# Turning two 64-wide heads with one 128x128 transposition, and moving the first key projections to other PSUM banks

## The chip, the cores and the metric

The kernel runs on one core of one Trainium2 chip. The metric is the time of one execution on the device in microseconds (us); what is compared is the median over runs of the same program.

## The reference

Two layers of an encoder block on 512 tokens of width 1024, all in float32. Each layer is a gated feed-forward, a token mixer, a second gated feed-forward, and a gated embedding step, with a layer norm after each. The change is inside the token mixer, and there in the gated delta rule with 4 heads of dimension 128, which works on chunks of 64 tokens:

```
gdn_qkv = silu(causal_dwconv(gdn_qkv, gdn_conv_w))      # 4 taps along the tokens
g_q = l2_normalize(g_q) * GDN_HEAD_DIM ** -0.5
g_k = l2_normalize(g_k)
...
u, w  = t_inv @ (v * beta), t_inv @ (k * beta * exp(gcum))
qk    = (q @ k.T) * decay
step:  v_new = u - w @ state
       o     = q_dec @ state + qk @ v_new
       state = state * g_last + k_dec.T @ v_new
```

The same mixer also holds a stick-breaking attention (4 heads of 64) and a short gated convolution; their outputs are concatenated and projected.

## The kernel before

**Number formats.** Every large product is done as three float16 products (`mm3`, lines 256 to 258): operands are split into a high and a low float16 half, and high x high, high x low and low x high are accumulated in PSUM. Weights arrive by DMA as float32 into `raw` (3 buffers) and are split by one ScalarE and one VectorE instruction per half tile (lines 139 and 140) into a buffer `w`.

**The mixer (`mix_body`).** Tokens are kept along the free dimension: `proj_T` computes a projection as 128 channels x 512 tokens in one PSUM bank, 24 matmuls of 512 columns each. For the delta rule each head's projection passes through `conv` (one ScalarE instruction, line 616, and three on VectorE, line 619), which reads the PSUM bank of the projection, and then through `silu` (ScalarE, line 546). The result has the head's 128 channels on the partitions and 512 tokens = 8 chunks of 64 on the free axis. The state update needs it the other way round, with tokens on the partitions. `turn` (line 700) does that for a pair of heads (`hp` names the pair, `e` the head in it): for each chunk, head 0 goes to partitions 0 to 63 and head 1 to partitions 64 to 127 of one PSUM tile, by a float32 matmul with the identity for each head and chunk, 16 matmuls per pair. There are six turns per layer: two for the keys (`pkt`), two for the values (`pvt`), two for the queries (`pqt`). Behind them ScalarE and VectorE read the turned tiles (lines 717, 718, 721 for keys; 949 for values; 962, 963 for queries).

Keys and queries stay in `kq`, since the products of a chunk with itself (`pm`, line 749, and `pqk`, line 976) and with the state (`pks`, line 1007) read them with channels on the partitions. Values live only until their turn: their `silu` is done in place in the buffer that `conv` filled.

**PSUM.** There are three pools: `acc` (2 banks, the output of `proj_T`), `bank` (3) and `bank2` (3). The first key projections (`early`, two heads, name `pk`) go to `acc`, as do the four `pv` products before them, the next two key projections, and the attention's projections `psb` behind those.

**SBUF.** In the mixer, pool `w1` has 5 buffers under the tag `w`; the split weights, the attention's `hl`, and `zT` share them. A load whose buffer is not free waits. `conv` tiles have 5 buffers under the tag `cv`.

**Order.** A planner orders every engine's instructions once, at compile time, by program order as priority and by its own estimates of when each will be ready. TensorE then runs its queue strictly in that order. The planner fills TensorE with whatever product is ready: around the key turns these are the `psb` matmuls, and around the value and query turns the next projection's matmuls and the steps of a triangular inverse (`levels`, line 916). A few places are tied by hand: `silu` waits for the last exponential before it (`tables_end`), to save loads of activation tables.

**The gate chain.** The gate values `g` go through a chain from `pab` (line 631) through VectorE and ScalarE to `pe` (line 654), then `pl` (line 672), the decays `E` and `ET`, and only then the first `silu` of the keys.

Of the kernel before, what the change touches and what calls it, by code (L numbers as in the profile page):

```python
# [10 lines left out]
F32 = mybir.dt.float32  # L11
# [6 lines left out]
P = 128  # L18
# [15 lines left out]
class Block:  # L34
# [511 lines left out]
        self.silu_end = self.nc.scalar.activation(out, a, AF.Silu, scale=scale)  # L546
        self.after(self.silu_end, self.tables_end)

    def proj_T(self, w, xT, c, name):

        ps = self.acc(name)
        for k in range(KD):
            self.mm3(
                ps, [w[:, h, k, c * P : (c + 1) * P] for h in range(2)],
                [xT[:, h, k] for h in range(2)], k == 0, k == KD - 1,
            )
        return ps

    def mix_body(self, i, j, last, pool):
        nc, ins, xT, x = self.nc, self.ins, self.xT, self.x  # L560
# [3 lines left out]
        H, C, NC, G16 = 4, 64, 2 * NT, NT * 4  # L564
        halves = [slice(64 * e, 64 * e + 64) for e in range(2)]
# [22 lines left out]
        ps = self.bank2("ps_rows", (P, 64))  # L588
# [24 lines left out]
        def conv(ps, c):  # L613
            a = pool.tile([P, S], F32, name="conv", tag="cv", bufs=5)
            w = lambda tap: cw[:, tap * 12 + c : tap * 12 + c + 1]
            nc.scalar.activation(a, ps, AF.Copy, scale=w(3))
            for tap in (2, 1, 0):
                d = 3 - tap
                nc.vector.scalar_tensor_tensor(
                    a[:, d:], ps[:, : S - d], w(tap), a[:, d:], op0=ALU.mult, op1=ALU.add  # L620
                )
            return a

        w = self.load_cols(w_in, OFF_K)
        early = [conv(self.proj_T(w, xT, e, "pk"), 4 + e) for e in range(2)]


        pab = self.bank("pab", (P, NT, 2, 4))
        for c in range(2):
            for e in range(2):  # L630
                nc.tensor.matmul(
                    pab[halves[e], :, c], self.ident[:, halves[c]], ab[:, :, e::2],
                    start=True, stop=True,
# [32 lines left out]
        for a in range(2):  # L666
# [13 lines left out]


        kq2 = [
            self.w2.tile([P, 2, NC, 2, C], F32, name="kq", tag="w") for _ in range(2)
        ]
        kq = [kq2[h // 2][:, h % 2] for h in range(H)]
        bv = self.w2.tile([P, NC, 2, P], F32, name="bv", tag="w")
        kdec = self.w2.tile([P, NC, 2, P], F32, name="kdec", tag="w")
        ssk = pool.tile([P, NC, 2], F32, name="ssk")
# [2 lines left out]
        def bc(cols, n=P):  # L691
            m = cols.shape[-1]
            return cols.rearrange("p (m a) -> p m a", a=1).to_broadcast([P, m, n])

        def turn(src, name):

            pts = [self.bank(name, (P, 4, P)) for _ in range(2)]
            for n in range(NC):
                for e in range(2):
                    nc.tensor.matmul(  # L700
                        pts[n // 4][halves[e], n % 4], src(e, n), self.ident, start=True, stop=True
                    )
            return [(pt, slice(4 * b, 4 * b + 4)) for b, pt in enumerate(pts)]

        def chunks(v):
            return v.rearrange("p (n c) -> p n c", c=C)

        for hp in range(2):
            if hp == 1:
                w = self.load_cols(w_in, OFF_K + 256)  # L710
            for e in range(2):
                h = 2 * hp + e
                a = conv(self.proj_T(w, xT, e, "pk"), 4 + h) if hp else early[e]
                self.silu(kq[h][:, :, 0], chunks(a))
            for pt, ns in turn(lambda e, n: kq[2 * hp + e][:, n, 0], "pkt"):
                sq = self.t2("sq", (P, 4, P))
                nc.scalar.activation(sq, pt, AF.Square)
                nc.vector.tensor_reduce(
                    ssk[:, ns, hp], sq, axis=mybir.AxisListType.X, op=ALU.add
                )  # L720
                nc.vector.tensor_tensor(
                    kdec[:, ns, hp], pt, bc(eg[:, 1].rearrange("p (n h) -> p n h", h=2)[:, ns, hp]),
                    op=ALU.mult,
                )
# [76 lines left out]
        for hp in range(2):  # L801
            ps = self.proj_T(wq, xT, hp, "psb")
            for e in range(2):
                own, other, h = rows_of(e), rows_of(1 - e), 2 * hp + e
# [4 lines left out]
        for hp in range(2):  # L809
            ps = self.proj_T(wk, xT, hp, "psb")  # L810
            for e in range(2):
                own, other, h = rows_of(e), rows_of(1 - e), 2 * hp + e
# [9 lines left out]
        for n_u, (h, kts) in enumerate(((0, (2, 3)), (0, (1,)), (1, (2, 3)), (0, (0,)), (1, (1,)), (2, (2, 3)),  # L822
                       (1, (0,)), (2, (1,)), (3, (2, 3)), (2, (0,)), (3, (1,)), (3, (0,)))):
            hp, e = divmod(h, 2)
            es = slice(64 * e, 64 * e + 64)
            off = {k: 256 * (k == 3) for k in kts}
            n = 512 if kts == (0,) else 384
            zb = self.bank2("zb")[:, :n]
            zt = {k: zb[:, off[k] : off[k] + S - k * P] for k in kts}
            for k in kts:  # L830
# [3 lines left out]
                    start=k == kts[0], stop=False, skip_group_check=True,  # L834
# [15 lines left out]
            pair = hlb[:, n_u % 4]  # L850
# [4 lines left out]
            for k in reversed(kts):  # L855
                for k2 in range(NT - 1, k - 1, -1):
                    lhs = self.ntri if k2 == k else self.nones
                    for q in range(2):
                        nc.tensor.matmul(
                            zt[k][:, (k2 - k) * P :], lhs, hls[h][k2][:, q], start=False,  # L860
                            stop=k2 == k and q == 1, skip_group_check=True,
# [5 lines left out]
            for k in kts:  # L867
# [3 lines left out]
                    start=k == 2, stop=k == 0, skip_group_check=True,  # L871
# [7 lines left out]
        hb, a = ([self.t2(n) for _ in range(2)] for n in ("hb", "sca"))  # L879
        for c in range(2):  # L880
            nc.scalar.activation(hb[c], self.proj_T(wh, xT, c, "psh"), AF.Copy, scale=IWS)
        for c in range(2):
# [3 lines left out]
            w = lambda tap: cw[:, 48 + 2 * tap + c : 49 + 2 * tap + c]  # L886
# [52 lines left out]
        level = levels()  # L939
        for hp in range(2):  # L940
            w = self.load_cols(w_in, OFF_V + 256 * hp)
            pair = []
            for e in range(2):
                next(level, None)
                a = conv(self.proj_T(w, xT, e, "pvv"), 8 + 2 * hp + e)
                self.silu(a, a)
                pair.append(chunks(a))
            for pt, ns in turn(lambda e, n: pair[e][:, n], "pvt"):
                nc.vector.tensor_tensor(bv[:, ns, hp], pt, bc(rk[:, 1, ns, hp]), op=ALU.mult)


# [1 line left out]
        for hp in range(2):  # L953
            w = self.load_cols(w_in, OFF_Q + 256 * hp)
            for e in range(2):
                h = 2 * hp + e
                next(level, None)
                a = conv(self.proj_T(w, xT, e, "pqq"), h)
                self.silu(kq[h][:, :, 1], chunks(a))
            for pt, ns in turn(lambda e, n: kq[2 * hp + e][:, n, 1], "pqt"):  # L960
                sq = self.t2("sq", (P, 4, P))
                nc.scalar.activation(sq, pt, AF.Square)
                nc.vector.tensor_reduce(
                    ssq[:, ns, hp], sq, axis=mybir.AxisListType.X, op=ALU.add
                )
# [17 lines left out]
        for hp in range(2):  # L983
            w = self.load_cols(w_in, OFF_Z + 256 * hp)
# [192 lines left out]
```

## Time and profile before

| | us |
|---|---|
| median of 3 runs | 2031.88 |
| lowest, highest run | 2029.93, 2032.16 |
| the profiled execution, its own time | 2031.65 |
| its span, first to last instruction | 2029.9 |

The profile shows one execution. What lies around the span is 1.75 us. TensorE appears as two rows, PE for the matmuls and PEld for the loading of the stationary operand; DVE is VectorE, ACT is ScalarE, POOL is GpSimd, and SPq is the queue that issues the DMAs. PEclk is the clock that TensorE was granted as a share of full speed, and over the whole span it is 0.997. A matmul's row shows its whole latency, so the spacing of starts, not the duration, is what one costs in a stream.

### The profile page before, as it was taken

Reading aid. Unit: us, or ns where it says so; the run is one execution under the profiler, and the core shown is the slowest. Engines: PE = TensorE matmul, PEld = TensorE weight load, DVE = VectorE, ACT = ScalarE, POOL = GpSimd, SP = SyncE. Lnnn points to the kernel's source line nnn. Section 1 sums busy time; section 2 is a strip of 40 time slices with the busy share of each in tenths; the row PEclk is TensorE's granted clock in tenths of the full one; section 3 lists DMA queues with packets and bytes.
Section 4 is the critical chain, followed back from the end, with each engine's and each line's share of the span. In section 5 each row is a group of like instructions: output and inputs, shape, how many; then the busy total and the mean of one; then the engine's idle time right before and its main releaser. Section 6 shows DMA issues by size and latency. Waiting matters only on the chain.

```text
span 2029.9 us, 33679 instructions
## 1 busy us (share of the span) xinstructions
PE 1983.4 (98%) x14346; PEld 1289.0 (64%) x14346; DVE 1523.3 (75%) x2347; ACT 874.2 (43%) x1295; POOL 64.0 (3%) x84
## 2 busy tenths in 40 slices
PE   7999999999999999999999999999999999999998
PEld 5677686545545686776467686855455466776853
DVE  7995866775479986958897867577755798967686
ACT  6453352454244453543364443434533354543431
POOL 1000000100000000000000000002000000000000
PEclk9999999999999999999999999999999999999999
DMA  7533320431044443433324333222311624433221
GB/s 218 195 112 107 97 85 1 126 77 63 1 167 124 126 127 106 121 104 125 125 80 129 104 119 89 64 65 66 94 42 43 207 64 146 125 104 84 94 73 42
DMA packets 245361, 205.19 MB, mean 101 GB/s; under 512 B 20846, under 2 KB 225500, under 8 KB 245212
## 3 DMA queue, kind: packets, MB, share of 16 engines
q1 hardware_dynamic: 245212, 203.05, 32.6%
q8 instruction: 112, 1.84, 0.4%
q14 instruction: 37, 0.30, 0.0%
HBM read 200.14 MB, written 2.88 MB: 100 GB/s over the span
## 4 chain that ended last, share of the span: by engine, by line
PE 79%; DVE 12%; ACT 5%; DMA 2%; issue 1%; SPq 1%; POOL 0%; DVEq 0%; ACTq 0%
PE po L258 7%; PE po L256 7%; PE po L257 7%; PE pA L256 6%; PE pA L258 6%; PE pA L257 6%; PE pB L258 3%; PE pB L257 3%; PE pB L256 3%; DVE wq L140 3%; DVE w L140 2%; ACT w L139 2%; ACT wq L139 1%; PE pC L258 1%; PE pC L256 1%; PE pC L257 1%
## 5 line engine op out<-in xcount | busy, mean ns | idle before, releaser
L140 DVE SCALAR_TENSOR_TENSOR wq<-f,wq 128x1024 f16<-128x1024 f32 (+1 forms) x240 | 333.9, 1395 | 19.0 <-ACT wq L139 15.7
L139 ACT ACTIVATE wq<-f 128x1024 f16<-128x1024 f32 (+1 forms) x240 | 279.5, 1191 | 126.1 <-PE pB L258 83.2
L139 ACT ACTIVATE w<-raw 128x1024 f16<-128x1024 f32 (+1 forms) x196 | 193.8, 1032 | 264.6 <-PE po L258 226.3
L256 PE MATMUL po<-w,hT 128*128 128x512 f16 x704 | 266.7, 379 | 3.7 <-ACT hT L286 1.5
L256 PE MATMUL pA<-xS,wq 128*128 128x256 f16 x960 | 261.6, 272 | 6.8 <-ACT up L407 5.3
L257 PE MATMUL po<-w,hT 128*128 128x512 f16 x704 | 266.5, 379 | 0.0
L258 PE MATMUL po<-w,hT 128*128 128x512 f16 x704 | 264.3, 379 | 1.9 <-DVE hT L287 1.9
L258 PE MATMUL pA<-xS,wq 128*128 128x256 f16 x960 | 261.6, 273 | 0.0
L257 PE MATMUL pA<-xS,wq 128*128 128x256 f16 x960 | 261.6, 273 | 0.0
L140 DVE SCALAR_TENSOR_TENSOR w<-raw,w 128x1024 f16<-128x1024 f32 (+1 forms) x196 | 230.0, 1193 | 36.4 <-ACT w L139 36.4
L257 PEld LDWEIGHTS <-wq 128*128 128x128 f16 x2240 | 219.1, 98 | 42.1 <-issue 11.7
L453 DVE TENSOR_TENSOR f<-f 128x512 f32<-128x512 f32 x320 | 218.4, 686 | 28.1 <-DMA f<-in_ffn_w_in 23.0
L256 PEld LDWEIGHTS <-wq 128*128 128x128 f16 x2240 | 219.1, 98 | 30.1
L258 PEld LDWEIGHTS <-wq 128*128 128x128 f16 x2240 | 219.1, 98 | 27.5
L472 DVE SCALAR_TENSOR_TENSOR x_tok<-po,x_tok 128x512 f32<-128x512 f32 x144 | 97.5, 685 | 82.4 <-PE po L258 82.3
L256 PEld LDWEIGHTS <-hT 128*128 128x128 f16 x704 | 68.8, 98 | 85.2 <-ACT hT L286 9.9
L258 PEld LDWEIGHTS <-hT 128*128 128x128 f16 x704 | 68.0, 98 | 84.8 <-DVE hT L287 5.3
L395 DVE TENSOR_TENSOR sg<-pB,sg 128x256 f32<-128x256 f32 x80 | 33.6, 420 | 117.5 <-PE pB L258 117.5
L257 PEld LDWEIGHTS <-hT 128*128 128x128 f16 x704 | 68.9, 98 | 76.9 <-issue 1.4
L392 ACT ACTIVATE sg<-pA 128x256 f32<-128x256 f32 x80 | 30.6, 382 | 194.1 <-PE pA L258 194.1
L257 PEld LDWEIGHTS <-w 128*128 128x128 f16 x640 | 62.9, 98 | 63.1 <-issue 16.4
L256 PEld LDWEIGHTS <-w 128*128 128x128 f16 x640 | 62.7, 98 | 61.4 <-issue 6.2
(289 smaller groups left out, 3872.0 us busy)
## 6 DMA issues: line engine op xcount, KB each, us to landing
f<-in_ffn_w_in SPq DMA_DIRECT2D x160, 512.0 KB, 5.1
raw<-in_ffn_w_out SPq DMA_DIRECT2D x44, 1024.0 KB, 6.1
raw<-in_mix_w_in SPq DMA_DIRECT2D x28, 1024.0 KB, 5.3
raw<-in_mix_w_out SPq DMA_DIRECT2D x8, 1024.0 KB, 4.9
raw<-in_ple_w_gate SPq DMA_DIRECT2D x8, 1024.0 KB, 7.5
raw<-in_ffn_w_in SPq DMA_DIRECT2D x6, 1024.0 KB, 5.0
ln_gb<-in_ln_g SPq DMA_DIRECT2D x8, 512.0 KB, 3.6
ln_gb<-in_ln_b SPq DMA_DIRECT2D x8, 512.0 KB, 5.1
```

Source lines behind the costliest of these rows:

```text
L139: self.nc.scalar.activation(hi, raw, AF.Copy, scale=WS),
L140: self.nc.vector.scalar_tensor_tensor(lo, raw, WS, hi, op0=ALU.mult, op1=ALU.subtract),
L256: nc.tensor.matmul(ps, a[0], b[0], start=first, stop=False, **k)
L257: nc.tensor.matmul(ps, a[0], b[1], start=False, stop=False, **k)
L258: nc.tensor.matmul(ps, a[1], b[0], start=False, stop=last, **k)
L392: nc.scalar.activation(half(new.sg, 1), new.A, AF.Copy)
L395: nc.vector.tensor_tensor(half(old.sg, 1), old.B, half(old.sg, 1), op=ALU.add)
L453: nc.vector.tensor_tensor(f[:, to], f[:, a], f[:, b], op=ALU.add)
L472: self.nc.vector.scalar_tensor_tensor(xs, po, scale, xs, op0=ALU.mult, op1=ALU.add)
```

## The change

Three things are edited.

1. `kq2`, which held two heads one after the other (head, chunk, key or query, token), is laid out as chunk, key or query, head, token. The two heads of a pair then lie side by side for each chunk: 128 adjacent columns. For the values a new tile `vp` of the same kind is taken from `w1`, tag `w`, one per pair, and `silu` writes there instead of in place.
2. `turn` issues one `nc.tensor.transpose` per chunk, on 128 columns, instead of two matmuls with the identity on 64 columns each. What lands in PSUM is the same, in the same place.
3. `proj_T` takes an optional `bank`, and the first two key projections go to `bank2` instead of `acc`.

```
-    def proj_T(self, w, xT, c, name):
-        ps = self.acc(name)
+    def proj_T(self, w, xT, c, name, bank=None):
+        ps = (bank or self.acc)(name)
...
-        early = [conv(self.proj_T(w, xT, e, "pk"), 4 + e) for e in range(2)]
+        early = [conv(self.proj_T(w, xT, e, "pk", self.bank2), 4 + e) for e in range(2)]
...
-            self.w2.tile([P, 2, NC, 2, C], F32, name="kq", tag="w") for _ in range(2)
+            self.w2.tile([P, NC, 2, 2, C], F32, name="kq", tag="w") for _ in range(2)
         ]
-        kq = [kq2[h // 2][:, h % 2] for h in range(H)]
+        kq = [kq2[h // 2][:, :, :, h % 2] for h in range(H)]
...
             pts = [self.bank(name, (P, 4, P)) for _ in range(2)]
             for n in range(NC):
-                for e in range(2):
-                    nc.tensor.matmul(
-                        pts[n // 4][halves[e], n % 4], src(e, n), self.ident, start=True, stop=True
-                    )
+                nc.tensor.transpose(pts[n // 4][:, n % 4], src(n), self.ident)
...
-            for pt, ns in turn(lambda e, n: kq[2 * hp + e][:, n, 0], "pkt"):
+            for pt, ns in turn(lambda n: kq2[hp][:, n, 0].rearrange("p e c -> p (e c)"), "pkt"):
...
-            pair = []
+            pair = self.w1.tile([P, NC, 2, C], F32, name="vp", tag="w")
             for e in range(2):
                 next(level, None)
                 a = conv(self.proj_T(w, xT, e, "pvv"), 8 + 2 * hp + e)
-                self.silu(a, a)
-                pair.append(chunks(a))
-            for pt, ns in turn(lambda e, n: pair[e][:, n], "pvt"):
+                self.silu(pair[:, :, e], chunks(a))
+            for pt, ns in turn(lambda n: pair[:, n].rearrange("p e c -> p (e c)"), "pvt"):
...
-            for pt, ns in turn(lambda e, n: kq[2 * hp + e][:, n, 1], "pqt"):
+            for pt, ns in turn(lambda n: kq2[hp][:, n, 1].rearrange("p e c -> p (e c)"), "pqt"):
```

## Rows read from the trace of the kernel before

**Rows 1.** The page, busy time by engine: us, share of the span, instructions.

```profile
PE 1983.4 (98%) x14346; PEld 1289.0 (64%) x14346; DVE 1523.3 (75%) x2347; ACT 874.2 (43%) x1295; POOL 64.0 (3%) x84
```

**Rows 2.** Windows: length; busy us of PE, PEld, DVE, ACT, POOL; PEclk, DMA, GB/s.

```profile
370.00:372.80 2.80, 0.70 (x10) 0.31 (x8) 2.77 (x6) 0.69 (x1) 0.00 (x0) 0.98 0.14 17
372.80:376.20 3.40, 3.39 (x9) 1.24 (x10) 3.17 (x8) 2.39 (x6) 0.00 (x0) 0.52 0.96 297
404.00:416.00 12.00, 12.00 (x59) 5.38 (x57) 5.23 (x16) 2.96 (x5) 4.77 (x4) 1.00 0.16 23
416.00:440.00 24.00, 23.41 (x123) 10.64 (x122) 21.92 (x47) 17.56 (x29) 0.00 (x0) 1.00 0.34 100
480.00:540.00 60.00, 60.00 (x582) 33.22 (x581) 28.03 (x39) 17.82 (x26) 0.00 (x0) 1.00 0.08 29
580.00:610.00 30.00, 28.63 (x165) 13.67 (x166) 21.26 (x36) 13.00 (x20) 2.21 (x3) 1.00 0.43 151
976.00:978.00 2.00, 2.00 (x19) 1.84 (x18) 2.00 (x3) 2.00 (x4) 0.00 (x0) 1.00 0.44 117
```

**Rows 3.** Timeline of PE, layer 1, around the second key pair's first projection.

```profile
370.29 0.41 PE L631 MATMUL pab<-ab,ident 128*64 128x16 f32 x8
372.81 0.61 PE L256 MATMUL pk<-xT,w 128*128 128x512 f16 x1 [2.11 <-DVE conv L619]
...
376.15 0.38 PE L258 MATMUL pk<-xT,w 128*128 128x512 f16 x1
...
378.53 0.29 PE L654 MATMUL pe<-g,uin 128*128 128x16 f32 x2
```

**Rows 4.** Timeline of PE, layer 2, the same place.

```profile
1376.52 0.39 PE L256 MATMUL pk<-xT,w 128*128 128x512 f16 x1 [1.11 <-DVE conv L619]
```

**Rows 5.** Chain that ended last, turns of layer 1: start us, us, what.

```profile
391.13 2.35 PE pkt L700 x32
393.48 0.32 PE psb L257
...
394.88 1.96 PE pkt L700 x29
...
490.02 0.58 PE pvt L700 x4
...
494.16 1.89 PE pvt L700 x28
```

**Rows 6.** Instructions of tile `pkt`: count, ns min/median/max, first and last start us, forms.

```profile
L700 PE MATMUL pkt<-ident,kq x128: 272/273/324, 391.1 to 1399.0; 128*64 128x128 f32 x128
```

**Rows 7.** Instructions of tile `ps_t`, the turned tokens elsewhere in the kernel.

```profile
L220 PE MATMUL ps_t<-ident,x_tok x256: 272/273/448, 4.7 to 1979.2; 128*128 128x128 f32 x128
L223 ACT ACTIVATE xT<-ps_t x64: 573/597/616, 5.8 to 1979.7; 128x512 f16<-128x512 f32 x64
```

**Rows 8.** Timeline of PE around one block of eight such transpositions.

```profile
1005.25 0.38 PE L258 MATMUL pgate<-w,xT 128*128 128x512 f16 x1
1005.47 1.04 PE L220 MATMUL ps_t<-ident,x_tok 128*128 128x128 f32 x8
1006.34 0.38 PE L256 MATMUL pp<-w,pT 128*128 128x512 f16 x1
```

**Rows 9.** Line 546, `silu`: count, ns min/median/max, first and last start us.

```profile
L546 ACT ACTIVATE kq<-conv x16: 613/629/631, 390.3 to 1541.5; 128x512 f32<-128x512 f32 x16
L546 ACT ACTIVATE conv<-conv x8: 629/629/630, 488.1 to 1511.5; 128x512 f32<-128x512 f32 x8
```

**Rows 10.** Timeline of PE at the end of the first value projection, layer 1.

```profile
489.64 0.38 PE L258 MATMUL pvv<-xT,w 128*128 128x512 f16 x1
```

**Rows 11.** Timeline of ACT, the next splits of weights after that.

```profile
556.29 3.90 ACT L139 ACTIVATE w<-raw 128x1024 f16<-128x1024 f32 x4
```

**Rows 12.** Timeline of DVE, the last step of `g`, layer 1.

```profile
376.52 0.17 DVE L646 TENSOR_TENSOR g<-g,nega 128x16 f32<-128x16 f32 x1
```

**Rows 13.** DMA issues: engine, count, KB each, median us to landing.

```profile
raw<-in_mix_w_out SPq DMA_DIRECT2D x8, 1024.0 KB, 4.9
```

## The prediction

> **What bounds the kernel now.** I read the page first: PE is busy for 98% of the span [rows 1], so an edit counts by what it does to PE's queue and by whether another engine is close behind it. The windows show that stage by stage, inside the mixer, where all edits are. In the value and query stretch PE has not one idle microsecond of 60 while DVE works 28 and ACT 18 [rows 2]: what is cut from PE there should come off the end. Elsewhere the cover is thinner. Behind the key turns PE is full for 12 us with DVE under half busy, but from 416 to 440 DVE is at 21.9 of 24 and PE already idles 0.6; from 580 to 610 PE idles 1.4 [rows 2]. Last, the one large wait: in layer 1 PE stands for 2.11 us before the second key pair, waiting for `conv` on DVE to let go of an `acc` bank, and runs the next matmuls at a granted 0.52 [rows 2, 3]. In layer 2 the same wait is 1.11 us, and no slow stretch follows it [rows 4].
>
> **Part 1, the turns.** `turn` issues 2 pairs x 8 chunks x 2 heads = 32 matmuls per name and layer, 64 in both; the trace holds 128 for `pkt` [rows 6]. So each float32 matmul with the identity is two PE instructions, and a turn is 32. `ps_t` is what the new form looks like: 64 tiles of four transpositions, and 256 instructions for these 256 [rows 7]: one each. A turn goes from 32 to 8.
>
> Old price, from the chain: a key turn in one piece holds PE 2.35 us, and the float16 matmul behind it takes 0.32 instead of 0.22, so 2.45. The second key turn has 29 of its instructions in 1.96, 0.0676 each, hence 2.16 for 32; more float32 work follows, so no dearer exit. A value turn runs in two pieces, 4 and 28 instructions: 0.58 + 1.89, and 0.10 at the exit, 2.57 [rows 5]. The other value and query turns repeat that pattern, four in all; the last is followed by float32 work, 0.10 less. Per layer: 2.45 + 2.16 + 4 x 2.57 - 0.10 = 14.8 us.
>
> New price: eight transpositions start at 1005.47, 0.22 behind the start of the float16 matmul ahead of them, which is that matmul's own spacing, and the next float16 matmul starts at 1006.34 [rows 8]. So they hold PE 0.87 us, without entry or exit. Six make 5.2. Twice per layer (`pm`, `pqk`) other float32 work now pays the 0.10 entry that the turn paid: 0.2. Saved: 14.8 - 5.2 - 0.2 = 9.4 us per layer, 18.8 in both.
>
> Bounds: the nearest row has the same type, the same 128 columns and the same identity, so the size is good to some tenths per turn; at 1.04 us, the time of the block with its tail [rows 8], it is 12 x 0.17 = 2.0 less, 16.8. Not better than 18.8, unless the planner also places things better.
>
> **What the clock does in a turn.** Sixteen transpositions (two such blocks) fill most of 976 to 978, and the clock granted there is 1.00 [rows 2]; the matmul behind the block of rows 8 starts on time. The Trainium skill, "TensorE: Matmul & The Clock Gate", section "Part 4: PE-mode transpose", says against this change that transpose mode does not count as busy for the clock gate, so that full clock does not engage in it. By this trace eight or sixteen in a row do not lower the granted clock; by the page, each turn might bring a stretch at the lower level. I take the trace and keep the other as a rival.
>
> **What the turns wait for.** A transposition needs both heads' `silu`, where the early 4 instructions needed only one. The 28 already wait for the second head, so the block sits where they sat and PE has nothing new to wait for; the 0.58 just disappears. The `silu` count is unchanged, and its duration is 629 ns both for values in place and for keys into a strided tile [rows 9], so 0. Readers of the turned tiles find the same layout: 0. No DMA is added and none is moved past another on SP's queue; POOL gets nothing.
>
> **The new tile.** `vp` takes one of five `w1` buffers, twice per layer. When the first value head's `silu` starts (488.1), the weights of both value pairs, both query pairs and the first z pair can hold all five, and the first to come free is that of the value projection whose last matmul starts at 489.64 [rows 9, 10] and ends at 490.02. `silu` could thus start 1.9 us later. Behind it on ACT stands the second head's first `conv` step, which waits for that same matmul; it can be pushed by one `silu`, 0.63 us, and then the second `silu` and the turn by as much. Worst case 0.6 per layer, 1.2 in all; nothing if the planner swaps the two; I take 0.6. Later takers are far off: the next split of weights comes at 556 [rows 11], when both `vp` are long free. The `conv` buffers come free earlier, which nothing here waits for.
>
> **Part 2, the banks.** With the first pair in `bank2`, the second pair's `acc` banks hold only `pv` results evicted long before, and the wait for `conv` goes: 2.11 us in layer 1, 1.11 in layer 2 [rows 3, 4]. Layer 1 also gets back the slow stretch: from 372.81 to 376.15 eight matmul spacings took 3.34 us at a granted 0.52, the lower of the two levels, 1.2 GHz [rows 2, 3]; at 0.215 each they take 1.72, so 1.62. Sum 2.11 + 1.62 + 1.11 = 4.8 us.
>
> What is late next there: `pe` needs `g`, which DVE finishes at 376.69 [rows 12]. PE reached `pe` at 378.53 [rows 3], some 20 matmuls, 4.3 us at full clock, behind the start of the second pair. If the planner leaves `pe` that far behind, PE now gets there at about 370.7 + 4.3 = 375.0 and stands 1.7 us, and in layer 2 most of the 1.1 comes back too. But it places by its own times, and 10 us of ready matmuls (two projections, 48 x 0.215) can stand ahead of `pe`. So 2 to 4.8, and I take 4.8. Were the cover gone, it would be 2.
>
> **Sum.** -18.8 - 4.8 + 0.6 = -23.0 us. The profiled execution took 2031.65 by its own time and 2029.9 by its span, the median of the runs is 2031.88, 0.2 above. So 2031.9 - 23.0 = 2008.9: 2009 us, in the profile a span near 2007.
>
> **Rivals.**
>
> *DVE becomes the bound behind the keys.* PE reaches 416 earlier by the two key turns and the wait: (2.45 - 0.87) + (2.16 - 0.97) + 3.7 = 6.5 us in layer 1 and 2.8 + 1.1 = 3.9 in layer 2. If the stretch at 21.9 of 24 on DVE [rows 2] cannot follow, up to 10.4 us come back as waits before the attention's products. For: DVE's share there. Against: from 404 to 416 DVE is idle 6.8 of 12 us [rows 2] and can take work earlier. Time if all is lost: 2019; half: 2014.
>
> *The wait moves to `pe`.* Part 2 gives 2 instead of 4.8: 2012; if it gives nothing, 2014.
>
> *The transpositions let the clock fall.* If each of 12 turns brought a stretch like the one after the 2.11 us wait, 1.62 us each, 19.4 us would be given back: 2028, inside what cannot be told from no change. Against: the granted 1.00 in rows 2.
>
> *Slower: the buffer pool pushes the output weights behind the state loop.* If the planner gives freed `w1` buffers to `vp` and lets the four `mix_w_out` tiles queue behind them, a tile that lands late is exposed on PE with a transfer of 4.9 us [rows 13] and its split, for which four ACT halves took 3.9 [rows 11], so some 2 for one tile: 7 us. One per layer is 14 and still leaves a gain; from 1.6 per layer (23 us) it decides, and two per layer give 2037. For: PE already idles 1.4 us between 580 and 610 [rows 2]. Against: the splits begin at 556, some 40 us after the last `vp` is free.
>
> **Chances.** As forecast, 2004 to 2012: 0.62. DVE bound behind the keys, 2012 to 2019: 0.13. Wait at `pe`, 2011 to 2014: 0.11. Clock: 0.04. Slower: 0.04. Better than 2004, because the new order also closes some of the small waits: 0.06. A difference of 0.2%, 4 us, is about what a measurement of this kernel can tell from no change. The first three and the last are all faster by more, 0.92; the clock rival is no change, 0.04; slower 0.04. The range takes in the first three cases and leaves out the tails: 2003 to 2020, of which the likeliest case alone is 2004 to 2012.
>
> **What the profile after should show.** One instruction per transposition: 96 under the three names on the line of `turn`, in blocks of 8 that hold PE 0.87 us, with float16 spacing on both sides. No early piece of 4. The second key pair starting within 0.3 us behind `pab` in both layers, with a granted clock of 1.00 after it. PE's matmul count down by 288. PE still full from the values to the queries, and that stretch shorter by some 6.6 us per layer. I would be wrong if PE waits longer for `g`, for `silu` at a turn, or for attention splits (`hl`) than now; a planner's order that has shifted elsewhere can add or take a few microseconds that none of these terms foresee.

## The result and the profile after

The changed kernel takes 2017.18 us in the median of 4 runs (2016.35 to 2021.14), against 2031.65 for the kernel before, measured beside it: a ratio of 0.9934, 95% interval 0.9917 to 0.9951. It is faster, and the time lies inside the range, but 8 us above the 2009 forecast. The profiled execution took 2017.74 by its own time, 2016.0 by its span; the pair of profiled executions differs by 13.9 us where the sum said 23.0. Nine microseconds are missing, and the rows show where to look.

The page after, busy time by engine, answers [rows 1]:

```profile
PE 1966.5 (98%) x14058; PEld 1274.0 (63%) x14058; DVE 1524.1 (76%) x2347; ACT 871.4 (43%) x1295; POOL 65.7 (3%) x84
```

PE has 288 matmuls less, as forecast, and 16.9 us less work. The span fell by 13.9 only, so PE idles 3.0 us more than before.

The timeline of PE around the first value turn answers [rows 5], the instructions of the tile `pkt` behind it [rows 6]:

```profile
491.51 0.38 PE L258 MATMUL pvv<-xT,w 128*128 128x512 f16 x1
491.73 1.06 PE L700 MATMUL pvt<-ident,vp 128*128 128x128 f32 x8
492.72 0.45 PE L914 MATMUL pq<-TU,Ms 64*64 64x64 f32 x8
```

```profile
L700 PE MATMUL pkt<-ident,kq x32: 272/273/329, 389.6 to 1389.9; 128*128 128x128 f32 x32
```

There is one instruction per transposition (32 in `pkt` over both layers, 96 under the three names), in one block of 8 per turn, with no early piece of 4 and no wait. But the block's price is 0.99 us from its start to the next matmul's start, not 0.87. Five of the six turns of a layer are followed by small float32 tiles (`pm`, `pq`, `pu`) and cost 0.99 to 1.02; the first, with a float16 matmul behind it, costs 0.93.

The timeline of PE at the second key pair, layer 1 and then layer 2, answers [rows 3, 4]. A bracket names the wait ahead of the row and who ended it:

```profile
370.51 0.41 PE L631 MATMUL pab<-ab,ident 128*64 128x16 f32 x8
370.86 0.39 PE L257 MATMUL pk<-xT,w 128*128 128x512 f16 x1
...
374.97 0.38 PE L258 MATMUL pk<-xT,w 128*128 128x512 f16 x1
376.93 0.37 PE L654 MATMUL pe<-g,uin 128*128 128x16 f32 x2 [1.58 <-DVE g L646]
...
1372.09 0.37 PE L654 MATMUL pe<-g,uin 128*128 128x16 f32 x2 [1.73 <-DVE g L646]
...
1373.30 0.63 PE L257 MATMUL pk<-xT,w 128*128 128x512 f16 x1
1373.73 0.63 PE L258 MATMUL pk<-xT,w 128*128 128x512 f16 x1
```

The second pair's first row starts 0.35 us behind `pab` (the row of its first matmul, one of L256, is missing from the trace): the bank wait is gone. PE then runs some 20 matmuls and stands at `pe` for `g`, 1.58 us in layer 1 and 1.73 in layer 2, where the slow stretch now follows (matmuls 0.43 apart). The windows show the clock there, and the stretches of [rows 2] (same columns):

```profile
1372.90:1376.30 3.40, 3.40 (x12) 1.43 (x12) 2.09 (x5) 0.91 (x2) 0.00 (x0) 0.52 0.61 158
...
416.00:440.00 24.00, 23.14 (x123) 10.67 (x122) 17.84 (x39) 14.83 (x26) 0.00 (x0) 1.00 0.43 109
480.00:540.00 60.00, 59.30 (x595) 33.86 (x589) 37.38 (x53) 22.66 (x33) 0.00 (x0) 1.00 0.22 71
```

Layer 1 lost its slow stretch and layer 2 got one. That PE waits longer for `g` is one of the signs by which the prediction said it would be wrong; a second came too, since PE's waits for `hl` at `zb` are 0.78 us per layer where they were 0.55. From 480 to 540 PE, full before, now idles 0.7 us. The timeline of DVE shows why `g` is late, and answers [rows 12]:

```profile
374.45 0.71 DVE L619 SCALAR_TENSOR_TENSOR conv<-pk,cw,conv 128x509 f32<-128x509 f32 x1
375.39 0.17 DVE L645 SCALAR_TENSOR_TENSOR g<-g,spa 128x16 f32<-128x16 f32 x1 [0.23 <-ACT spa L644]
375.49 1.22 DVE L140 SCALAR_TENSOR_TENSOR w<-raw,w 128x1024 f16<-128x1024 f32 x1
376.62 0.17 DVE L646 TENSOR_TENSOR g<-g,nega 128x16 f32<-128x16 f32 x1
```

DVE ends `g` at the same moment as before (376.79, before 376.69). Its order in this stretch is unchanged: halves of weight splits (L140) stand ahead of the gate's steps, one even between the last two steps of `g`. A new bank on PE's side can't bring `g` forward.

One more wait is new, in both layers, in the sinks' stage right behind the key turns. PE's timeline in layer 1:

```profile
401.48 0.38 PE L256 MATMUL psb<-xT,w 128*128 128x512 f16 x1 [1.04 <-DVE qs L804]
```

PE reaches the third `psb` projection before DVE has evicted `qs` (moved it out of its bank). DVE is busy 4.8 of the 5.0 us from 396.5 to 401.5. Before the change PE did not wait here.

Where the time came from is best read in three stretches of each mixer. Worked out from the starts of tiles in each trace (first `pv`, first `psb`, first `zb`, last `pot`), in us, layer 1 / layer 2:

| kernel | keys: pv to psb | psb to zb | zb to last pot | median of its runs |
|---|---|---|---|---|
| before | 40.1 / 37.5 | 27.7 / 27.7 | 188.7 / 188.7 | 2031.65 |
| changed | 37.8 / 39.5 | 26.3 / 26.3 | 183.5 / 183.5 | 2017.18 |
| turns alone (e1) | 40.5 / 39.8 | 26.3 / 26.3 | 183.6 / 183.6 | 2020.65 |
| banks alone (e2) | 38.8 / 36.8 | 27.7 / 27.7 | 188.7 / 188.7 | 2031.44 |
| gate ahead (e3) | 36.0 / 36.0 | 26.2 / 26.2 | 183.6 / 183.6 | 2013.54 |
| own tile (e4) | 38.4 / 39.1 | 26.3 / 26.3 | 184.0 / 184.0 | 2020.96 |
| each turn twice (e5) | 38.3 / 37.0 | 27.1 / 27.1 | 187.0 / 187.0 | 2024.74 |
| pairs by matmul (e6) | 38.3 / 36.8 | 27.2 / 27.2 | 187.3 / 187.3 | 2026.58 |
| gate ahead, no banks (e7) | 36.3 / 36.3 | 28.0 / 29.3 | 183.6 / 183.5 | 2019.00 |
| gate ahead, psb banks (e8) | 36.0 / 36.0 | 25.2 / 25.2 | 186.2 / 185.3 | 2015.26 |
| gate ahead, own tile (e9) | 36.0 / 36.0 | 26.2 / 26.2 | 184.0 / 184.0 | 2013.83 |
| before, gate ahead (e10) | 36.3 / 36.3 | 28.3 / 28.3 | 191.0 / 191.0 | 2033.42 |

In the pair before and changed, the two stretches behind the keys give 6.6 us per layer, 13.2 together: this is the turns. The key stretch gives 0.3 over both layers (77.6 to 77.3): this is what came of the banks. (The kernel before had medians of 2032.38, 2032.57 and 2031.98 in the three sets of experiments; each ratio below is against its own.)

### The profile page after: what moved, and what is told of

The parts are those of the page before. It is cut to its first block, busy times and chain, and to the rows that moved or that the text cites. A ratio compares the mean times of both kernels' runs of the same rounds, so it can differ in the third digit from the quotient of the medians.

```text
span 2016.0 us, 33100 instructions
## 1 busy us (share of the span) xinstructions
PE 1966.5 (98%) x14058; PEld 1274.0 (63%) x14058; DVE 1524.1 (76%) x2347; ACT 871.4 (43%) x1295; POOL 65.7 (3%) x84
## 4 chain that ended last, share of the span: by engine, by line
PE 74%; DVE 14%; ACT 7%; DMA 2%; issue 2%; SPq 1%; POOL 0%; DVEq 0%; ACTq 0%
PE po L258 7%; PE po L256 7%; PE po L257 7%; PE pA L256 6%; PE pA L257 6%; PE pA L258 6%; DVE w L140 3%; PE pB L258 3%; PE pB L257 3%; PE pB L256 3%; DVE wq L140 2%; ACT w L139 2%; ACT wq L139 2%; PE pC L258 1%; PE pC L257 1%
## 5 line engine op out<-in xcount | busy, mean ns | idle before, releaser
L140 DVE SCALAR_TENSOR_TENSOR wq<-f,wq 128x1024 f16<-128x1024 f32 (+1 forms) x240 | 333.9, 1394 | 19.0 <-ACT wq L139 15.7
L256 PE MATMUL po<-w,hT 128*128 128x512 f16 x704 | 266.7, 379 | 3.0 <-ACT hT L286 0.9
L256 PE MATMUL pA<-xS,wq 128*128 128x256 f16 x960 | 261.6, 273 | 6.9 <-ACT up L407 5.5
L140 DVE SCALAR_TENSOR_TENSOR w<-raw,w 128x1024 f16<-128x1024 f32 (+1 forms) x196 | 229.4, 1193 | 37.4 <-ACT w L139 37.4
L256 PEld LDWEIGHTS <-wq 128*128 128x128 f16 x2240 | 219.1, 98 | 30.1
L256 PEld LDWEIGHTS <-hT 128*128 128x128 f16 x704 | 68.8, 98 | 84.7 <-ACT hT L286 9.4
```

The source lines that it names most:

```text
L140: self.nc.vector.scalar_tensor_tensor(lo, raw, WS, hi, op0=ALU.mult, op1=ALU.subtract),
L256: nc.tensor.matmul(ps, a[0], b[0], start=first, stop=False, **k)
```

## The experiments

My theory after the result: the turns pay as a count of instructions, less one new wait on DVE; the banks pay little because `g` sits behind weight splits on DVE. Rivals: turns whose clock falls, the new `vp` tile as the cost, banks without worth of any kind.

**e1, turns alone**: the early key projections back in the ring of before.

```diff
-        early = [conv(self.proj_T(w, xT, e, "pk", self.bank2), 4 + e) for e in range(2)]
+        early = [conv(self.proj_T(w, xT, e, "pk"), 4 + e) for e in range(2)]
```

> The transpositions and the paired layout alone; the first key projections stay in acc. Theory: in the changed kernel the wait for a PSUM bank did not go, it moved to pe, which waits for g (1.58 and 1.73 us where conv cost 2.11 and 1.11), so the banks are worth about nothing and this kernel takes the time of the changed one, 2017 us, within 2; its profile has the waits for conv on pk again (about 2.1 and 1.1 us) and none on pe. Rival: the banks are worth the 4.8 us of the prediction and the turns fell short by all that is missing: 2022 us.

**e2, banks alone**: the kernel before, with that line and the `bank` argument of `proj_T` from the change.

> The kernel before with the first key projections in bank2 and nothing else. Theory: the order on VectorE is that of before, so g is ready no earlier; PE waits at pe for 1.5 to 1.8 us in both layers; time as before, 2031.5 us, within 2. Rival: 4.8 us less, 2027 us.

e1 took 2020.65 us (2016.6 to 2021.7), ratio 0.9936 [0.9922, 0.9949], which can't be told from the ratio of the whole change. Its median lies 3.7 us above the theory and 1.4 below the rival, and its five runs spread over 5 us, so e1 alone does not decide between them. e2 does: 2031.44, ratio 0.9997 [0.9989, 1.0006], no gain that can be told from none, and at most 2.2 us, not 4.8. PE's timeline of e1 in both layers, then of e2:

```profile
374.10 0.51 PE L256 MATMUL pk<-xT,w 128*128 128x512 f16 x1 [2.37 <-DVE conv L619]
...
1372.96 0.39 PE L256 MATMUL pk<-xT,w 128*128 128x512 f16 x1 [3.08 <-DVE conv L619]
```

```profile
378.18 0.36 PE L654 MATMUL pe<-g,uin 128*128 128x16 f32 x2 [2.59 <-DVE g L646]
```

Without the banks PE waits for `conv`, with them for `g`: one wait in two places. (In layer 2 of e2 it is 0.55 us, so my 1.5 to 1.8 for both layers was wrong.) By the key stretch the banks gave 2.0 us against before (e2) and 3.0 against e1, over both layers, in single traces; and the wait for `conv` alone is 1.1 to 3.1 us long in the two traces that have it, so such differences are small beside its own spread.

The rows also show what that spread follows. A row of ACT in the changed kernel and the row of DVE behind it; then a row of ACT and one of PE in layer 2 of the kernel before:

```profile
367.31 1.06 ACT L139 ACTIVATE w<-raw 128x1024 f16<-128x1024 f32 x1 [1.05 <-DMA raw<-in_mix_w_in]
368.40 1.23 DVE L140 SCALAR_TENSOR_TENSOR w<-raw,w 128x1024 f16<-128x1024 f32 x1 [0.69 <-ACT w L139]
```

```profile
1370.92 1.06 ACT L139 ACTIVATE w<-raw 128x1024 f16<-128x1024 f32 x1 [1.04 <-DMA raw<-in_mix_w_in]
1380.64 0.29 PE L654 MATMUL pe<-g,uin 128*128 128x16 f32 x2
```

ACT's split stands until the transfer of its weights lands, DVE's half of the split waits for ACT's, and `conv` and `g` stand behind it on DVE. In both layers of the changed kernel, the one before, e1, e2, e4, e5 and e6, DVE ends `g` 9.48 to 9.49 us after the start of that ACT split. With the new banks PE takes `pe` 9.62 to 9.63 us after it in all ten stretches, though the wait is anything from 0.52 to 2.82 us long. In the old ring PE takes the second pair 5.60 to 5.61 us after it in all four, and `pe` 9.72 after it where no slow stretch came between, 11.3 to 11.4 where one did. So in this order of DVE the landing of one weight transfer sets when PE goes on. The new banks bring `pe` forward by 0.1 us per layer, and by the 1.6 us of a slow stretch where the old ring happened to have one.

**e3, gate ahead**: the changed kernel, with the splits of the last two of the four weight tiles loaded ahead put behind the gate's last step on ACT (`Ln`) and on DVE (`g`).

```diff
-        ahead = [self.load_cols(w_in, c) for c in (0, 256, OFF_SC + 512, OFF_SC + 256)]
+        ahead = [self.load_cols(w_in, c) for c in (0, 256)]
+        ahead += [
+            self.load_cols(w_in, c, behind=(g_act, g_dve)) for c in (OFF_SC + 512, OFF_SC + 256)
+        ]
```

> The changed kernel, with the splits of the last two of the four weight tiles loaded ahead tied behind the last steps of g on ScalarE and VectorE. Theory: g is late since a split that waits for its transfer stands ahead of it on VectorE; with it out of the way g is ready 2 to 3 us earlier, the wait at pe is gone (1.58 and 1.73 us) and the stretch at the lower clock after it in layer 2 as well (1.7 us): 5 us less than the changed kernel, 2012 us. Rival: what is saved at pe is waited for at the next place (pl, the silu of the keys, or psb): 2016 to 2018 us.

It took 2013.54 us (2013.22 to 2013.74), 1.5 us above the theory and clear of the rival, ratio 0.9906 [0.9893, 0.992]; run again as e11, 2012.70 (2012.45 to 2012.93), 0.9905 [0.9891, 0.9919]. It beats both kernels, and its runs lie within 0.5 us where those of the changed kernel spread over 4.8. The timelines of DVE and of PE:

```profile
373.13 0.74 DVE L621 SCALAR_TENSOR_TENSOR conv<-pk,cw,conv 128x510 f32<-128x510 f32 x1
373.79 0.17 DVE L648 TENSOR_TENSOR g<-g,nega 128x16 f32<-128x16 f32 x1
...
376.15 2.35 DVE L142 SCALAR_TENSOR_TENSOR w<-raw,w 128x1024 f16<-128x1024 f32 x2
```

```profile
371.48 0.41 PE L633 MATMUL pab<-ab,ident 128*64 128x16 f32 x8
371.82 0.39 PE L259 MATMUL pk<-xT,w 128*128 128x512 f16 x1
...
374.20 0.29 PE L656 MATMUL pe<-g,uin 128*128 128x16 f32 x2
```

`g` ends at 373.96, ahead of the splits, and PE takes `pe` 2.7 us behind `pab` (6.4 and 6.6 in the changed kernel) with no wait and no slow stretch. The key stretch is 36.0 in both layers: 5.3 us less than the changed kernel's 77.3 over both. The split that waited for its transfer is one of those that were moved. The edit moves splits on ACT and on DVE together, so their shares are not told apart.

**e7, gate ahead without the banks**, and **e10, gate ahead in the kernel before**: the same order with the ring of before, the second also with the turns of before.

> The kernel with the two later splits of weights put behind the gate, but with the first key projections back in the ring of before. Theory (it is the weight splits on VectorE that stand ahead of both the convolution and the gate, and the other banks only choose which of the two is waited for): the splits' delay is gone from the convolutions too, the wait of the second key pair is under 1 us a layer, and the time is 2013.5 to 2015.5. Rival (the banks and the order are both needed): the second pair waits for the first convolution as before, about 2 us a layer more than with the banks, 2017.5 or above.

> The kernel before, with only the two later splits of weights put behind the gate: turns and banks as before. Theory (the order pays where the banks let TensorE reach the gate early; without them the wait for a free bank moves from the second key pair to psb, as in the same order without the banks): 1.5 us faster than before, 2030 to 2032. Rival (the order is a gain of its own, and the changed kernel's banks have little to do with it): 4 us or more below before, under 2028.5.

e7 took 2019.00 us (2018.56 to 2019.34), ratio 0.9938 [0.9925, 0.995]; e10 2033.42, 1.0007 [0.9998, 1.0015]. In e7 the wait at the second pair is gone, as the theory said, but the time is the rival's, 5.5 us above e3. PE's timeline of e7, then of e10:

```profile
1388.67 0.61 PE L258 MATMUL psb<-xT,w 128*128 128x512 f16 x1 [2.75 <-DVE conv L621]
```

```profile
416.14 0.39 PE L258 MATMUL psh<-xT,w 128*128 128x512 f16 x1 [1.99 <-DVE kl L820]
```

In the old ring the bank is waited for one step later, at `psb`, in both layers. In e10 the key stretch is 5.1 us shorter over both layers, and all of it and some more is given back behind it: 0.6 before `zb` and 2.3 after, per layer. My theory for e10 (2030 to 2032) missed by 1.4 us, its rival by 5. The order and the banks pay together, each alone does not.

**e5, each turn twice**: every transposition issued twice into the same place. **e6, pairs by matmul**: the same pairs turned by an ordinary float32 matmul with the identity.

```diff
-                nc.tensor.transpose(pts[n // 4][:, n % 4], src(n), self.ident)
+                nc.tensor.matmul(
+                    pts[n // 4][:, n % 4], src(n), self.ident, start=True, stop=True
+                )
```

> The changed kernel with every one of its 96 transpositions issued twice into the same place. Theory (a transposition costs its 0.109 us of TensorE each and nothing else): 96 more of them, 8 x 0.109 = 0.87 us a turn, 12 turns, +10.5 us against the changed kernel's 2017.2, about 2027.6, and the granted clock stays at 1.00 in the stretch of each turn. Rival (activity in transpositions lets the clock fall): blocks of 16 longer than 1.75 us, rows of 0.43 us for the matmuls behind them, over 2032.

> The changed kernel with each 128x128 transposition written as an ordinary float32 matmul with the identity (two instructions instead of one, same operands and same place): the pairing alone, without the transpose mode. Theory (pairing halves the columns' passes and the mode halves them again): the blocks hold 8 x about 0.21 = 1.7 to 2.0 us instead of 0.87 to 1.0, +0.85 to 1.1 us a turn, 12 turns, 2027 to 2030. Rival (pairing gives it all, the mode nothing): within 2 us of the changed kernel's 2017.2.

e5 took 2024.74 us, ratio 0.9967 [0.9956, 0.9979]; e6 2026.58, 0.9972 [0.9962, 0.9983]. PE's timeline in e5, the window of that turn (columns as above), then PE's timeline in e6:

```profile
493.15 1.94 PE L701 MATMUL pvt<-ident,vp 128*128 128x128 f32 x16
495.01 0.50 PE L915 MATMUL pq<-TU,Ms 64*64 64x64 f32 x9
```

```profile
493.20:495.00 1.80, 1.80 (x17) 1.64 (x16) 0.69 (x1) 0.00 (x0) 0.00 (x0) 1.00 0.91 315
```

```profile
492.76 2.02 PE L700 MATMUL pvt<-ident,vp 128*128 128x128 f32 x16
494.71 0.50 PE L916 MATMUL pq<-TU,Ms 64*64 64x64 f32 x9
```

Sixteen transpositions run at a granted 1.00 and hold PE 1.86 us, eight more for 0.87: 0.109 each. e5 came out below its 2027.6 for reasons that the trace shows. The 1.04 us wait at `psb` is gone in it, in both layers, which leaves 8.4 of the 10.5; and its key stretch, which varies, is 2.0 us shorter than the changed kernel's, which leaves 6.4 (the spans of the two traces differ by 6.6, the medians by 7.6). e6 lies 0.4 us below its range. Behind the keys the sums close. From the changed kernel to e5 the six blocks of a layer grow from 6.0 to 11.25 us, less 1.04 for the wait makes 4.2; the two stretches behind the keys grew by 4.3. To e6 the blocks grow to 11.76, less 1.04 makes 4.7; measured 4.7. From before to e6 they shrink from 13.77 to 11.76, 2.0; measured 1.9. So pairing alone gives 1.9 us per layer, and one instruction instead of two the other 4.7.

**e4, own tile**, and **e9, gate ahead with the own tile**: `vp` in a buffer of its own.

```diff
-            pair = self.w1.tile([P, NC, 2, C], F32, name="vp", tag="w")
+            pair = pool.tile([P, NC, 2, C], F32, name="vp", tag="vp", bufs=1)
```

> The changed kernel, with vp in a buffer of its own instead of one of the five that the weights share. Theory: the weights of the second value pair are split early again (about 436 instead of 485 us into the span), and the 0.55 us that PE waits for them in each layer goes: 1 us less, 2016 us, barely to be told from the changed kernel. Rival: the late loads cost more than that wait shows, by crowding ACT and DVE between 480 and 510: 3 us or more, 2014 us or less.

> The kernel with the two later splits of weights behind the gate, and the value pair vp in a buffer of its own instead of a slot of the weights' pool. With the gate in time the key stretch doesn't vary any more, so the slot's price can be read. Theory (pvv's wait of 0.55 us a layer for the weights' split is the slot's price): 2013.5 - 1.1 = about 2012.4. Rival (the pool's slots only set when weights are loaded, and what pvv gains the sinks' stage gives back, as the own buffer did before): 2013.5 or up to 1 us more.

e4 took 2020.96 us, ratio 0.9945 [0.9933, 0.9958]; the 2016 of my theory and the 2014 of its rival were both wrong. e9 took 2013.83 (2013.16 to 2014.81) beside 2012.70 for e3's form on the same chip (e11): the rival. PE's wait of 0.55 us for a weight split at `pvv`, present in every run with the shared slot, is gone in both, and the stretch from `zb` to the last `pot` is still 0.4 to 0.5 us longer (184.0). The slot in `w1` costs nothing in the end.

> The kernel with the two later splits of weights behind the gate, once more, as the mark for the one with vp in its own buffer on the same chip: 2013.5 within 0.5.

e11 came in 0.8 us below, 0.3 outside what was expected.

**e8, psb in other banks** on top of e3.

```diff
-            ps = self.proj_T(wq, xT, hp, "psb")
+            ps = self.proj_T(wq, xT, hp, "psb", self.bank2)
```

> The same splits behind the gate, the other banks kept, and the first two query projections of the sinks' stage (psb from wq) in the other banks too. Theory (TensorE's 0.8 to 1.0 us wait for VectorE's eviction of qs is a wait for a free bank): it goes in both layers, 2013.5 - 1.8 = about 2011.7. Rival (TensorE then stands later, at zb or at psb's next tile, for the same VectorE or ScalarE work): 2013.5 within 0.7.

It took 2015.26 us, ratio 0.9917 [0.9904, 0.9931], 1.7 us above e3 and so worse than both expected. PE's timeline, then DVE's:

```profile
412.69 0.47 PE L258 MATMUL psh<-xT,w 128*128 128x512 f16 x1 [1.98 <-DVE kl L818]
```

```profile
410.75 0.56 DVE L849 TENSOR_SCALAR sp<-zb 128x384 f32<-128x384 f32 x1 [1.30 <-PE zb L843]
411.94 0.69 DVE L818 SCALAR_TENSOR_TENSOR kl<-psb,ks 64x512 f16<-64x512 f32 x1
```

The wait for `qs` is gone, and a longer one for `kl`, a later eviction on DVE, takes its place. DVE is not short of time there: it idles 3.0 us before 405.3, and 1.30 us at `sp`, a step that waits for PE's `zb` and stands ahead of `kl`. The rows point to the order on DVE again, not to its load; no run tests this. In e10 `kl` stands behind the same step, which waits 1.62 us there.

## Why the prediction was right in direction and too large

The time fell inside the range since the range took in the first rivals; the likeliest case, 2004 to 2012, did not come. The term of the turns was too large, and the term of the banks came to almost nothing.

**Turns, -18.8 and +0.6 forecast, -13.2 measured** (6.6 per layer against 9.1). The mechanism was right; the sizes were off in three places. The old price: 13.77 us per layer in the trace of before, by the distance from the start of each piece to the next matmul's start, against 14.8; I had added 0.10 for an exit to nearly every turn, though the distances hold it already, and scaled turns that run among other small tiles up to 32 instructions at full price. The new price: 6.0 against 5.4 with the neighbours' entries, since a block ahead of small float32 tiles costs 1.0. The "1.04 us, the time of the block with its tail" that I gave as a bound was nearer than the 0.87 that I took. And 1.04 per layer came back as the wait at `psb`. Together 2.7 per layer, which with the +0.3 of `vp` that did not come is 2.4 of the 2.5 missing. The value and query stretch, which was to be 6.6 shorter, is 5.2 shorter from `zb` to `pot`.

**The wait at `psb`** is my first rival in small: "DVE becomes the bound behind the keys". I looked for it from 416 to 440, where DVE was at 21.9 of 24 [rows 2]; it came at 401, just ahead of a stretch (404 to 416 before the change) that I held for safe. It gave back 2.1 of the 10.4 us that were at stake; e5 and e6, in which PE is later, show none of it, and e8 that another bank only moves it.

**`vp`, +0.6 forecast, nothing measured** (e9). The `pvv` wait looks like its price and isn't.

**Banks, -4.8 forecast, -0.3 in the pair of profiles.** Here the choice failed, not the view: `g` at 376.69, `pe` reached at 375.0, 1.7 us of standing, all of it was in the text, and PE reached `pe` at about 375.3 and stood 1.58. I took 4.8 since the planner "places by its own times" and could put ready matmuls ahead; it left `pe` 20 matmuls behind, as before. The second rival, "the wait moves to `pe`", is what happened, and more of it than I allowed for: I left 2 us to the banks even so, and the traces leave 0.1 us per layer and the luck of a slow stretch. That luck explains the pair of profiles: the slow stretch of layer 1 went, and one as long came in layer 2. What I had not looked at are the rows ahead of `g` on DVE: the split that waits for its transfer, and another of 1.22 us between the last two steps of `g`. e3 shows that with those splits out of the way the key stretch is 5.6 us shorter than before (77.6 to 72.0), slightly more than the 4.8. So the gain was there, behind the order of the splits.

**The clock in a turn.** The granted clock is 1.00 over the 8 transpositions of a turn and over 16 in a row (e5), at 0.109 us each. The rival that rests on the Trainium skill, "TensorE: Matmul & The Clock Gate", section "Part 4: PE-mode transpose", is not borne out by any run here. The slow stretches that I read stood behind waits.

**The output weights** pushed behind the state loop, the slower rival: no wait of PE for a split or a transfer of theirs stands in the trace after, in either layer.

Open: why the stretch from `zb` to `pot` is longer by 0.4 to 0.5 us with the own tile. In e8 (1.8 to 2.6 longer than in e3) and e10 (2.3 longer than before) most of it is the wait of 1.98 to 1.99 us at `psh`; the rest is not taken apart, since the planner orders the whole stage anew in each of these kernels. Open too is why the weight transfer lands earlier or later beside PE's work, and what decides whether a slow stretch follows a wait. That the spread of the changed kernel's runs comes from these two is argued, since each kernel has one trace; e3's narrow spread fits it.

## What to carry over

When a wait on a bank is taken away, find the next thing that PE needs in that stretch and read who stands ahead of its producer on the producer's queue: here 1.2 us weight splits, not urgent, one of them waiting for a transfer, stood ahead of a 0.17 us step that PE waited for, and moving them was worth another 3.6 to 4.5 us between the medians. Price a block of short instructions by the distance from its start to the next instruction's start, with the neighbour that it really has. And a wait shown at an instruction is not yet a cost: take it away (e4, e8, e9) before counting on it.

## What the hardware showed

- The float32 product with the identity is two instructions and the transposition one, at nearly the same price per instruction: 16 hold PE 1.95 us in e6 and 1.86 in e5. An instruction that turns 64 columns costs 0.0675 us (28 in 1.89) and one that turns 128 costs 0.109, so joining two halves saves a fifth of their time, not half.
- The length of a wait on PE does not decide whether a slow stretch (3.4 us at a granted 0.50 to 0.52, the level of 1.2 GHz) follows it. One followed waits of 1.73 us (changed, layer 2), 1.98 (e8, layer 1), 2.11 (before, layer 1), 2.37 (e1, layer 1) and 2.75 (e7, layer 2). None followed waits of 1.58 (changed, layer 1), 1.98 (e8, layer 2), 2.75 (e7, layer 1), 2.82 (e4, layer 2) and 3.08 (e1, layer 2).
